# Laying the rows of five matmul operands without gaps in a one-core decoder layer

## The chip, the cores and the metric

The kernel runs on one NeuronCore of a Trainium2 chip. A core has a matrix engine (TensorE, "PE" in the profile, with its weight loads as "PEld"), a vector engine (VectorE, DVE), a scalar engine (ScalarE, ACT), a general engine (GpSimd, POOL), a synchronising engine that issues most transfers (SyncE, SP), and 16 DMA engines. On-chip memory (SBUF) has 128 partitions; matmul results go to PSUM, in banks of 512 float32 columns. The metric is the device time of one execution in microseconds.

## The reference

One decoder layer over 16 learned meta tokens and 256 tokens of width 2048, all in float32:

```python
h = jnp.concatenate([meta, x], axis=1)
h = h + hybrid_mixer(rmsnorm(h, norm_mix_g), w_in, ...)
h = h + squared_relu_mlp(rmsnorm(h, norm_mlp_g), w_ff1, w_ff2)
return rmsnorm(h, final_norm_g)[:, N_META:]
```

`hybrid_mixer` projects the normalised rows with `w_in` (13,336 columns: queries, keys and values of two branches, their gates, a forget gate). One branch is causal softmax attention with a forgetting term (8 heads of 128), the other a gated linear attention in chunks of 64 (4 heads, keys 256, values 512) with a normalisation by head and a SiLU gate. Each branch goes through its own output matrix and a sigmoid gate, the two are added, and `w_out` projects the sum:

```python
y = sigmoid(gate_fox) * (o_fox @ w_o_fox) + sigmoid(gate_gla) * (o_gla @ w_o_gla)
return y @ w_out
```

The MLP is `square(relu(xn @ w1)) @ w2` with 8192 hidden columns. The weights are most of the 289 MB that the kernel reads, and nearly all of the work is dense matrix products of 256 or 272 columns with them.

## The kernel before, in words

Everything is transposed: features lie on the 128 partitions, tokens along the free dimension. A vector of 2048 features is 16 row tiles of 128 partitions (`KT = 16`), and row tile k of an operand is the slice `[:, k, ...]` of one SBUF tile.

**Split operands.** A float32 number is cut into a high part, which the matmul type float32r (F32R) holds exactly, and a low part, the rest. An operand row tile holds its 256 high columns and then its 256 low columns, 512 in a row (`x[:, k]`). Weights are cut the same way. The product of one block of 128 output features is the function `gemm2`: for each of its 16 row tiles `mac2` issues two matmuls, the high weights against all 512 columns (L136) and the low weights against the 256 high columns (L137), all into one PSUM bank. The halves of the bank are added when it is read out. Each of these matmuls loads its own 128x128 weights first (PEld), while the matmul before it still runs.

**Weights.** `next_weights` fetches the next block of 128 columns in two halves of 512 KB (tile `raw`, SP's queue, L118), ACT copies each to the high part `whi` (L120) and DVE makes the low part `wlo` (L121), 1024 columns at a time. `raw`, `whi` and `wlo` have five buffers each. The blocks come in one fixed stream in the order of use, and a planner in the tile framework orders the instructions of each engine, from the order of the code.

**Operands.** The first operand, the normalised input, is the tile `x_row`. It holds 544 columns a row tile, `[meta high 16 | high 256 | low 256 | meta low 16]`; `x` is the 512 columns in the middle, `x_hi` the first 272 and `x_lo` the last 272. `gemm_all` multiplies all 272 token columns (L153 and L154 on `x_hi`, L155 on `x_lo` with its output 16 columns further on in PSUM). Five later operands come from the helper `operand`:

- `og` (L460, 16 row tiles), the output of the gated linear attention, and `x2` (L846), the normalised input of the MLP, both in the slot with tag "s2";
- `of` (L685, 8 row tiles, with `at=32`), the output of the softmax attention;
- `y` (L836), the gated sum, and `a` (L886), the squared ReLU of one quarter of the hidden columns, both in the slot with tag "s1", which `x_row` used before them.

The layout of such a tile is set by three lines:

```python
row = 2 * NT + 32                                       # 544
t = t[:, at:].rearrange("p (k r) -> p k r", r=row)
return t[:, :, 16 : 16 + 2 * NT].rearrange("p k (o t) -> p k o t", t=NT)
```

Row tiles are 544 columns apart, 2176 bytes, and each has its 512 columns after 16 unused ones and before 16 unused ones, as `x` has in `x_row`.

**Stages.** A first stage multiplies seven blocks while the input still arrives (`products`, L345 to L352), with the same row tile against several blocks in turn. Then come the four heads of the linear attention and the eight heads of the softmax attention, which read `x` and `x_hi`; then, for each pair of output blocks, gates on `x`, one block on `of` and two on `og`. `y` is split after that (`split_to`) and multiplied by `w_out`, and `x2` is written block by block as the residual grows. The MLP runs in four groups: 16 blocks on `x2` make one `a`, 16 blocks on `a` are added to the residual. The last four blocks of the last group are done in another order, so that the final normalisation of one half of the tokens can run beside the other half's products: first the low weights (L912), with the high weights kept in `whi_last` (tag "s2"), and then each half of 128 tokens with its high and low columns, 256 together (L928).

Of the kernel before, what the change touches and what calls it, by code (L numbers as in the profile page):

```python
# [8 lines left out]
F32R = mybir.dt.float32r  # L9
# [7 lines left out]
P = 128  # L17
# [3 lines left out]
NT = 256  # L21
# [44 lines left out]
def trunk(ctx: ExitStack, tc: tile.TileContext, hT, w_small, w_all, consts, w_alpha2, out):  # L66
# [3 lines left out]
    def nm(s):  # L70
        serial[0] += 1
        return f"{s}_{serial[0]}"
# [52 lines left out]
    def next_weights(keep_hi=None):  # L125
        c = chunk[0]
        chunk[0] += 1
        parts = []
        for i in range(2):
            hi, lo, step = weight_half(c, i, None if keep_hi is None else keep_hi[:, HK * i : HK * (i + 1), :])  # L130
            step(0, HK)
            parts.append((hi, lo))
        return lambda k: (parts[k // HK][0][:, k % HK, :], parts[k // HK][1][:, k % HK, :])
# [5 lines left out]
    def gemm2(w, x, k0=0, nk=KT):  # L139

        ps = bank(pg, "ps")
        for k in range(nk):
            hi, lo = w(k0 + k)
            mac2(ps, hi, lo, x[:, k], k == 0, k == nk - 1)
        issued()
        return ps
# [18 lines left out]
    def total(ps, t=None):  # L165

        b = tmp.tile([P, NT], F32, tag="evb", name=nm("evb"))
        nc.scalar.copy(b, ps[:, NT:512])  # L168
        if t is None:
            t = tmp.tile([P, NT], F32, tag="evt", name=nm("evt"), bufs=4)  # L170
        nc.vector.tensor_tensor(t, ps[:, 0:NT], b, op=ALU.add)  # L171
        return t
# [44 lines left out]

    def operand(pool, name, nk=KT, at=0, **kw):


        row = 2 * NT + 32
        t = pool.tile([P, at + nk * row], F32R, name=nm(name), **kw)
        t = t[:, at:].rearrange("p (k r) -> p k r", r=row)
        return t[:, :, 16 : 16 + 2 * NT].rearrange("p k (o t) -> p k o t", t=NT)


    h = keep.tile([P, KT, NA + 3], F32, name="h")
# [88 lines left out]
    for s in range(KT // 2):  # L316
# [5 lines left out]
        for kk in range(2):  # L322
            k = 2 * s + kk
# [15 lines left out]
        at = [(w[0][:, c], w[1][:, c]) for w, n in ((wa, 4), (wb, 3)) for c in range(n)]  # L339
# [118 lines left out]
    def og_tile():  # L458
        if not og_box:
            og_box.append(operand(keep, "og", tag="s2"))  # L460
        return og_box[0]
# [221 lines left out]
    branches = ExitStack()  # L683
    late = branches.enter_context(tc.tile_pool(name="late", bufs=1, reuse_waits="tile"))
    of = operand(late, "of", FOX_H, 32)  # L685
    negc = late.tile([P, FOX_H, NA], F32, name="negc")
    nc.gpsimd.dma_start(negc.rearrange("p h t -> p (h t)"), fdram.to_broadcast([P, FOX_H * NA]))
# [138 lines left out]
    for j0 in range(0, KT, 2):  # L826
        gates = ahead if j0 == 0 else [gate() for _ in range(4)]
        w = next_weights()
        for j in range(2):
            t = total(gemm2(w, of, k0=8 * j, nk=8))  # L830
            nc.vector.tensor_tensor(gates[2 * j], gates[2 * j], t, op=ALU.mult)
        for j in range(2):
            t = total(gemm2(next_weights(), og))
            nc.vector.tensor_tensor(t, gates[2 * j + 1], t, op=ALU.mult)
            nc.vector.tensor_tensor(yf[:, j0 + j, :], gates[2 * j], t, op=ALU.add)
    y = operand(keep, "y", tag="s1")  # L836
    for j in range(KT):
        split_to(y[:, j, 0, :], y[:, j, 1, :], yf[:, j, :])
# [220 lines left out]
```

## Time and profile before

| | |
|---|---|
| timed runs | 1597.07 us median of 3 (1596.95 to 1597.44) |
| span of the profiled execution | 1595.0 us |
| PE busy | 1585.0 us, 9812 matmuls |
| PEld busy | 1428.8 us |
| DVE, ACT, POOL busy | 1060.4, 790.8, 125.2 us |
| HBM read | 289.32 MB, 183 GB/s over the span |
| granted TensorE clock, mean | 0.998 |

The profile describes one execution, from its first instruction to its last; the timed runs count 2.1 us more than that span. A line of a group names the source line, the engine, the operation and the tiles (output, then inputs), the shape, how many there are, the sum of their durations, the mean of one in ns, and the idle time before them. In the chain and the timeline a row is a start, a length, and what ran. The ends of matmuls are modelled and overlap the next one, so durations of matmuls add up to more than the time they occupy; the starts give the pace. `x` in a group's name can be the tile `x` or the tile `x2`, since numbers in names are left out.

### The profile page before, as it was taken

The numbers are of one execution on the slowest core, as the hardware profiler recorded it, in microseconds if no ns is written. First come the engines' busy times: TensorE is split into PE (matmuls) and PEld (weight loads), VectorE is DVE, ScalarE is ACT, GpSimd is POOL, SyncE is SP. The second block draws the span as 40 slices with busy tenths as digits, with TensorE's granted clock in tenths as the row PEclk, the third lists the DMA queues.
The fourth block names the chain that finished last, engine by engine and source line by source line (L and its number), as shares of the span: only waits on it lengthen the run. The fifth ranks groups of instructions, "written<-read, shape, count | busy, mean of one in ns | idle before, by whom it ended". The sixth has DMA issues, their size and how long they took to land.

```text
span 1595.0 us, 25427 instructions
## 1 busy us (share of the span) xinstructions
PE 1585.0 (99%) x9812; PEld 1428.8 (90%) x9812; DVE 1060.4 (66%) x1659; ACT 790.8 (50%) x1271; POOL 125.2 (8%) x213
## 2 busy tenths in 40 slices
PE   9999999999999999999999999999999999999997
PEld 8999999999998888888888888888888888888887
DVE  7897757676655555555777776567655776567655
ACT  6665444454455444444555544444444444444563
POOL 6011000011100000000011000000000000000022
PEclk9999999999999999999999999999999999999999
DMA  9444545454445555555555555555555555555552
GB/s 323 156 164 155 180 157 183 167 188 164 159 167 181 191 186 189 189 191 187 186 195 186 188 193 187 188 191 190 187 190 190 186 189 193 186 188 193 186 183 97
DMA packets 86602, 293.09 MB, mean 184 GB/s; under 512 B 9112, under 2 KB 16800, under 8 KB 86352
## 3 DMA queue, kind: packets, MB, share of 16 engines
q1 hardware_dynamic: 85872, 289.62, 53.8%
q8 instruction: 77, 1.26, 0.3%
q0 software_dynamic: 176, 1.12, 0.2%
q10 hardware_dynamic: 432, 0.72, 0.1%
q14 instruction: 45, 0.37, 0.1%
HBM read 289.32 MB, written 2.11 MB: 183 GB/s over the span
## 4 chain that ended last, share of the span: by engine, by line
PE 99%; DMA 0%; issue 0%; POOL 0%; ACT 0%; DVE 0%; SPq 0%; POOLq 0%; ACTq 0%
PE ps L136 51%; PE ps L137 27%; PE psa L155 5%; PE psa L154 5%; PE psa L153 5%; PE ps L345 1%; PE ps L350 1%; PE ps L928 1%; PE pa L548 1%; PE ps L912 0%; DMA raw<-w_all_dram 0%; PE po L611 0%; POOL o L976 0%; PE po L188 0%; PE ps L348 0%
## 5 line engine op out<-in xcount | busy, mean ns | idle before, releaser
L121 DVE TENSOR_TENSOR wlo<-raw,whi 128x1024 fp32r<-128x1024 f32 x522 | 641.0, 1228 | 452.8 <-ACT whi L120 449.4
L120 ACT CAST whi<-raw 128x1024 fp32r<-128x1024 f32 x522 | 548.1, 1050 | 660.0 <-PE ps L136 493.1
L136 PE MATMUL ps<-x,whi 128*128 128x512 f32 x1952 | 683.8, 393 | 0.0
L137 PE MATMUL ps<-x,wlo 128*128 128x256 f32 x1952 | 548.5, 281 | 0.0
L136 PEld LDWEIGHTS ps<-x,whi 128*128 128x128 f32 x1952 | 366.1, 188 | 80.4
L137 PEld LDWEIGHTS ps<-x,wlo 128*128 128x128 f32 x1952 | 368.3, 189 | 0.1
L136 PE MATMUL ps<-a,whi 128*128 128x512 f32 x960 | 334.3, 392 | 0.0
L137 PE MATMUL ps<-a,wlo 128*128 128x256 f32 x960 | 269.1, 281 | 0.0
L136 PEld LDWEIGHTS ps<-a,whi 128*128 128x128 f32 x960 | 179.8, 188 | 39.9
L137 PEld LDWEIGHTS ps<-a,wlo 128*128 128x128 f32 x960 | 181.1, 189 | 0.3
L153 PE MATMUL psa<-x,whi 128*128 128x272 f32 x624 | 181.2, 290 | 0.0
L155 PE MATMUL psa<-x,whi 128*128 128x272 f32 x624 | 181.1, 290 | 0.0
L154 PE MATMUL psa<-x,wlo 128*128 128x272 f32 x624 | 179.4, 288 | 0.0
L153 PEld LDWEIGHTS psa<-x,whi 128*128 128x128 f32 x624 | 118.1, 189 | 0.4
L154 PEld LDWEIGHTS psa<-x,wlo 128*128 128x128 f32 x624 | 117.4, 188 | 0.0
L155 PEld LDWEIGHTS psa<-x,whi 128*128 128x128 f32 x624 | 117.2, 188 | 0.0
L136 PE MATMUL ps<-og,whi 128*128 128x512 f32 x256 | 89.6, 392 | 0.0
L136 PE MATMUL ps<-y,whi 128*128 128x512 f32 x256 | 89.1, 392 | 0.0
L854 POOL TENSOR_TENSOR acc<-acc,hsq 128x256 f32<-128x256 f32 x26 | 28.5, 1097 | 769.2 <-ACT hsq L853 769.2
L137 PE MATMUL ps<-og,wlo 128*128 128x256 f32 x256 | 71.9, 281 | 0.0
L137 PE MATMUL ps<-y,wlo 128*128 128x256 f32 x256 | 71.8, 281 | 0.0
L171 DVE TENSOR_TENSOR evt<-ps,evb 128x256 f32<-128x256 f32 x158 | 65.9, 418 | 0.5 <-ACT evb L168 0.5
(301 smaller groups left out, 1437.0 us busy)
## 6 DMA issues: line engine op xcount, KB each, us to landing
raw<-w_all_dram SPq DMA_DIRECT2D x537, 512.0 KB, 3.6
raw<-w_all_dram SPq DMA_DIRECT2D x8, 384.0 KB, 6.6
h<-hT_dram SPq DMA_DIRECT2D x8, 275.0 KB, 6.7
negc<-fdram POOLq DMA_DIRECT2D x1, 1088.0 KB, 8.0
out_dram<-o SPq DMA_DIRECT2D x2, 512.0 KB, 2.7
raw<-w_all_dram SPq DMA_DIRECT2D x2, 256.0 KB, 3.9
room<-w_small_dram SPq DMA_DIRECT2D x1, 320.0 KB, 7.4
out_dram<-o ACTq DMA_DIRECT2D x1, 320.0 KB, 3.1
```

Of the source, the lines that this page charges most:

```text
L120: nc.scalar.copy(hi[:, k, :], r)
L121: nc.vector.tensor_tensor(lo[:, k, :], r, hi[:, k, :].bitcast(F32), op=ALU.subtract)
L136: nc.tensor.matmul(ps, hi, x, start=first, stop=False)
L137: nc.tensor.matmul(ps[:, 0:NT], lo, x[:, 0, :], start=False, stop=last)
L153: nc.tensor.matmul(ps[:, 0:NA], hi, x_hi[:, k], start=(k == 0), stop=False)
L154: nc.tensor.matmul(ps[:, 0:NA], lo, x_hi[:, k], start=False, stop=(k == KT - 1))
L155: nc.tensor.matmul(ps[:, X_LO], hi, x_lo[:, k], start=False, stop=(k == KT - 1), skip_group_check=True)
L171: nc.vector.tensor_tensor(t, ps[:, 0:NT], b, op=ALU.add)
L345: nc.tensor.matmul(ps, hi, x[:, k], start=st, stop=False)
L350: nc.tensor.matmul(ps[:, 0:NT], lo, x[:, k, 0], start=False, stop=sp)
L548: nc.tensor.matmul(dst, k[:, a], q[:, a, :], start=(a == 0), stop=(a == 1))
L854: nc.gpsimd.tensor_tensor(acc, acc, sq, op=ALU.add)
```

## The change

The five operands keep their slots, but their row tiles now lie one behind the other, 512 columns (2048 bytes) apart, with nothing between them. The 32 spare columns for each row tile stay allocated at the tile's end. `at` still moves the first row of `of` by 32 columns. With the addresses that the tiles get, every row tile of the five now stands 448 bytes from the weight tiles, modulo 512; before, the row tiles of an operand stood 0, 128, 256 and 384 bytes from them in turn. `x_row` is not touched, nor is any instruction other than in its addresses.

```diff
     def operand(pool, name, nk=KT, at=0, **kw):
 
-
-        row = 2 * NT + 32
-        t = pool.tile([P, at + nk * row], F32R, name=nm(name), **kw)
-        t = t[:, at:].rearrange("p (k r) -> p k r", r=row)
-        return t[:, :, 16 : 16 + 2 * NT].rearrange("p k (o t) -> p k o t", t=NT)
+        t = pool.tile([P, nk * (2 * NT + 32)], F32R, name=nm(name), **kw)
+        return t[:, at : at + nk * 2 * NT].rearrange("p (k o t) -> p k o t", o=2, t=NT)
```

## The prediction

> **What bounds the kernel now.** I read the chain that ended last first, then the PE waits, then one long stretch of plain matrix products. The chain, by engine and by line, on the page:
>
> ```profile
> PE 99%; DMA 0%; issue 0%; POOL 0%; ACT 0%; DVE 0%; SPq 0%; POOLq 0%; ACTq 0%
> PE ps L136 51%; PE ps L137 27%; PE psa L155 5%; PE psa L154 5%; PE psa L153 5%; PE ps L345 1%; PE ps L350 1%; PE ps L928 1%; PE pa L548 1%; PE ps L912 0%; DMA raw<-w_all_dram 0%; PE po L611 0%; POOL o L976 0%; PE po L188 0%; PE ps L348 0%
> ```
>
> TensorE is the path from end to end, and 78% of it is the two matmuls of `mac2`, L136 (512 columns, high weights) and L137 (256 columns, low weights). The whole list of waits of that engine is three lines, 2.4 us together:
>
> ```profile
> PE warm L311 <- DVE ones L195: 1.3, 1, 1.3
> PE pn L952 <- ACT sq L933: 0.7, 1, 0.7
> PE ps L345 <- ACT whi L280: 0.4, 1, 0.4
> ```
>
> So no wait can be saved; only the pace of the matmuls can move the time. The stretch from 880 to 1560 us holds nothing but L136 and L137. Its busy times by engine (PE, PEld, DVE, ACT, POOL, then granted clock, DMA share, GB/s), and the matmul groups in it:
>
> ```profile
> 880.00:1560.00 680.00, 680.00 (x3907) 598.14 (x3906) 444.06 (x629) 321.28 (x456) 11.71 (x9) 1.00 0.56 189
> L136 PE MATMUL ps<-x,whi 128*128 128x512 f32 x999 | 348.2, 392 | 0.0
> L136 PE MATMUL ps<-a,whi 128*128 128x512 f32 x954 | 332.2, 392 | 0.0
> L137 PE MATMUL ps<-x,wlo 128*128 128x256 f32 x999 | 280.7, 281 | 0.0
> ```
>
> 999 + 954 = 1953 pairs in 680 us: 348.2 ns a pair. The durations 392 and 281 add up to 673, so each record is (673 - 348.2)/2 = 162 ns longer than the time until the next matmul starts. I therefore read any matmul duration as "start to next start, plus 162": L136 takes 230 ns, L137 119 (together 349). The clock is full (1.00), so the pace is not throttled. DVE, ACT and DMA are busy 65%, 47% and 56% of the stretch: if TensorE ran some per cent faster they would keep up.
>
> **The change, part by part.** Nothing is added, removed or reordered: every engine's list of instructions and waits is the same in both programs. What differs is where the rows of five tiles lie. The built programs place the weight tiles (`whi`, `wlo`) 128 bytes into a 512-byte period, and their rows are 512 bytes, so they stay there. The tiles `y`, `a`, `og`, `x2` begin 64 bytes into the period, `of` 448. Before, a row began 64 bytes in (128 more for `of`) and rows were 2176 bytes apart, so row k stood 128k bytes from the weights: 0, 128, 256, 384, 0 and so on. After, rows are 2048 bytes apart with no offset, so all stand at 64 - 128 = -64, that is 448. `x` is a tile of its own kind and keeps its places.
>
> The pairs that read the five tiles, first ones after 870 us (where "x" is `x2`), then the mixer's:
>
> ```profile
> L136 PE MATMUL ps<-x,whi x1024: 388/393/395, 871.0 to 1495.1; 128*128 128x512 f32 x171
> L136 PE MATMUL ps<-a,whi 128*128 128x512 f32 x960 | 334.3, 392 | 0.0
> L136 PE MATMUL ps<-og,whi 128*128 128x512 f32 x256 | 89.6, 392 | 0.0
> L136 PE MATMUL ps<-y,whi 128*128 128x512 f32 x256 | 89.1, 392 | 0.0
> L136 PE MATMUL ps<-of,whi 128*128 128x512 f32 x128 | 45.1, 393 | 0.0
> ```
>
> 1024 + 960 + 256 + 256 + 128 = 2624 pairs, 2624 x 348.2 ns = 913.7 us of the span. One nanosecond a pair is 2.6 us. That product is the whole sum; the question is its price.
>
> The trace of before has no 512-column matmul at distance 448, so I bound the price by the nearest rows. First, `x_hi` in `gemm_all`: its rows stand at 448, 64, 192, 320. Rows k = 12 and 13 of one such product, single instructions, 272 columns each (duration minimum/median/maximum):
>
> ```profile
> L153 PE MATMUL psa<-x,whi x1: 285/285/285, 286.7 to 286.7; 128*128 128x272 f32 x1
> L154 PE MATMUL psa<-x,wlo x1: 288/288/288, 286.9 to 286.9; 128*128 128x272 f32 x1
> L155 PE MATMUL psa<-x,whi x1: 292/292/292, 287.0 to 287.0; 128*128 128x272 f32 x1
> L153 PE MATMUL psa<-x,whi x1: 288/288/288, 287.1 to 287.1; 128*128 128x272 f32 x1
> L154 PE MATMUL psa<-x,wlo x1: 287/287/287, 287.2 to 287.2; 128*128 128x272 f32 x1
> L155 PE MATMUL psa<-x,whi x1: 289/289/289, 287.4 to 287.4; 128*128 128x272 f32 x1
> ```
>
> By distance: 448 gives 285 and 288, 0 gives 292, 64 gives 288 and 287, 128 gives 289. So 448 averages 286.5, the distances of before (multiples of 128) 290.5: 4 ns less a matmul. But L155 also writes PSUM 64 bytes further on, so this is an upper end of the gain: 8 ns a pair, 21 us.
>
> Second, runs of 256-column matmuls near the end, in the chain (start, length, count):
>
> ```profile
> 1562.51 5.68 PE ps L912 x48
> ...
> 1571.96 7.47 PE ps L928 x64
> ```
>
> L912 reads `a` against `wlo`, at multiples of 128: 5.68/48 = 118.3 ns. L928 reads `a` against `whi_last`, which begins 64 bytes into the period, so its distances are 64, 192, 320, 448: 7.47/64 = 116.7 ns. That is 1.6 ns less a matmul off the multiples of 128, with weights and rows in other absolute places than above.
>
> Third, against it: runs that stay at one distance for four matmuls, in the first stage (rows at 128, then 0, weights of other columns):
>
> ```profile
> 26.02 0.92 PE ps L345 x4
> 26.94 0.47 PE ps L350 x4
> 27.41 0.94 PE ps L345 x4
> 28.35 0.47 PE ps L350 x4
> ```
>
> (0.92 + 0.47 + 0.94 + 0.47)/8 = 350.0 ns a pair, 1.8 above the mixed rows.
>
> So the price lies between -8 and, at the cost of one bad distance for ever, the excess of 292 over the six rows' mean (288.2): 3.8 a matmul, +7.6 a pair. I take -1.6 a matmul, -3.2 a pair, from L912 against L928: these rows have the operands, the shape and the loads of weights of L137, and the single rows at 448 lie on the same side. 2624 x 3.2 = 8.4 us less.
>
> Edits that go together with it: L912 moves to 448 (64 x -1.6 = -0.1 us), and L928 moves to distance 0, since `whi_last` and `a` then both stand at 64 (128 x 1.6 = +0.2 us): nothing together. The ACT and DVE instructions that write the rows change addresses alone; TensorE waits for ACT 1.1 us in all, above, so whatever happens to them lies beside the matmuls. The pools keep their sizes but for `of`, 128 bytes shorter, which shifts its neighbours; the small matmuls are about 1% of the chain (L548 with L188 and L611 above, 16 us); I put them at nothing, and a tenth more or less on all of them would be 1.6 us either way.
>
> The span of the profiled execution is 1595.0 us; the timed runs have 1597.07 at the median, 2.1 us more for what lies around the span. 1595.0 - 8.4 = 1586.6 on the profile, about 1588.7 on the clock of the runs.
>
> **A rule against it.** "TensorE: Matmul & The Clock Gate" of the Trainium skill (Part 2, step-by-step) says that the engine reads the moving rows and the weights through two independent ports, and that loading the next weights takes no read bandwidth from the running matmul. By that rule the distance cannot matter and the time stays 1597. The rows above agree only in part: 285 to 292 for one shape at full clock is a spread by something, but it does not show that the two reads collide.
>
> **The rivals.** *No change.* If the spread is bookkeeping, no place is better. A duration here is a difference of two starts; a matmul that starts late lends its delay to the one before. The two triples above sum to 285 + 288 + 292 = 865 and 288 + 287 + 289 = 864, equal, though their distances differ: this speaks for it. Against it: 118.3 and 116.7 are means over long runs, where nothing can be lent. Time: 1597, within 3 us.
>
> *Slower.* What collides now in one row of four would collide in every one. Before, four distances take turns, and a bad one is paid once in four pairs; after, the engine settles into one relation of row and weights and pays or saves it 2624 times. The third fence is its price: +1.8 a pair, 4.7 us, 1601.8; at the worst distance seen, 7.6 a pair, 20 us, 1617. It decides from 1.2 ns a pair (3.2 us). For it: the only runs at a constant distance are the slower ones, and the 512-column shape never stood off a multiple of 128, so a cost of reading a long row from there has had no chance to show. Against it: neither of the two runs is at 448, and 448 has the shortest row of the six.
>
> **How the numbers follow.** 0.2% (3.2 us) is about what a measurement of this kernel can tell from no change. The forecast, faster by 3 to 21 us, gets 0.48: two kinds of rows in different absolute places point to it. Slower gets 0.36, since the step from four distances to one and from 272 to 512 columns is not covered by a row. No change gets 0.16, from the equal triples. The likeliest case alone is 1580 to 1593; with both signs holding much of the chance the range is 1580 to 1610, where the top leaves the dearest distance out and the bottom the full 8 ns a pair, about 0.1 each.
>
> **What would show it.** In the changed kernel's stretch from 880 to 1560 us the pairs should be 345 ns apart instead of 348.2 (some 18 more pairs in 680 us), with L136 near 390 and L137 near 279 by mean duration, and no difference left between one row and the next. Pairs of `x` in the mixer should stay as they are. L928 should move from 116.7 to about 118. The PE waits should stay at 2.4 us. I am wrong if pairs of `y`, `a`, `og` and `x2` are at or above 348 ns; if they stand at 350 or more, the constant distance is what costs, and if only L136 grows, it is the long row at an odd place.

## The result, and the profile after

The changed kernel takes 1610.12 us at the median (1609.51 to 1610.36) against 1597.03 us (1596.95 to 1597.44): a ratio of 1.0082, 95% interval 1.0069 to 1.0095. It is slower by 13.1 us. Its profiled execution has a span of 1608.3 us; before it was 1595.0 us, so the span shows the same 13.3 us.

The page's chain by engine, then the whole list of waits of TensorE (tile, line, what it waited for, us in total, times, longest), both of the changed kernel. Its lines below the helper stand three lower than before: L342 was L345, L909 was L912, L925 was L928.

```profile
PE 99%; DMA 0%; issue 0%; POOL 0%; ACT 0%; DVE 0%; SPq 0%; POOLq 0%; ACTq 0%
```

```profile
PE warm L308 <- DVE ones L195: 1.3, 1, 1.3
PE pn L949 <- ACT sq L930: 0.7, 1, 0.7
PE ps L342 <- ACT whi L277: 0.2, 1, 0.2
```

TensorE is still the whole path, and it waits 2.2 us where it waited 2.4. Nothing new makes it wait; it is its pace that fell. The same stretch as before, 880 to 1560 us, as a row of busy times by engine (PE, PEld, DVE, ACT, POOL, then granted clock, DMA share, GB/s):

```profile
880.00:1560.00 680.00, 680.00 (x3852) 590.59 (x3851) 436.97 (x622) 313.38 (x444) 8.94 (x7) 1.00 0.58 186
```

and the groups of matmuls in it (count, busy us, mean duration in ns, idle us before them):

```profile
L136 PE MATMUL ps<-x,whi 128*128 128x512 f32 x1008 | 356.4, 397 | 0.0
L136 PE MATMUL ps<-a,whi 128*128 128x512 f32 x917 | 323.9, 397 | 0.0
L137 PE MATMUL ps<-x,wlo 128*128 128x256 f32 x1008 | 283.2, 281 | 0.0
L137 PE MATMUL ps<-a,wlo 128*128 128x256 f32 x917 | 257.0, 281 | 0.0
```

1008 + 917 = 1925 pairs in 680 us are 353.2 ns a pair, where 1953 pairs were 348.2. The clock is full in both, and TensorE has no idle time before these matmuls in either. By the starts of the matmuls the extra 5.0 ns lie at 4.2 in L136 (235.0 ns to the next start, 230.8 before) and 0.8 in L137 (118.3, 117.5 before), and every row tile of `og`, `y`, `x2` and `a` has the same gaps. 2624 pairs x 5.0 ns = 13.1 us: that is the whole difference. The pairs on `x` keep 348.3 ns. Two of the chain's rows near the end (start, length, count), for the final blocks:

```profile
1575.47 5.66 PE ps L909 x48
...
1584.92 7.68 PE ps L925 x64
```

5.66/48 = 117.9 ns (118.3 before) and 7.68/64 = 120.0 ns (116.7 before): the first went from four distances to 448 and became slightly faster, the second from four distances to 0 and became slower.

### The profile page after: what moved, and what is told of

Read it like the earlier page. It is cut to its first block, busy times and chain, and to the rows that moved or that the text cites. A ratio compares the mean times of both kernels' runs of the same rounds, so it can differ in the third digit from the quotient of the medians.

```text
span 1608.3 us, 25427 instructions
## 1 busy us (share of the span) xinstructions
PE 1598.3 (99%) x9812; PEld 1430.4 (89%) x9812; DVE 1060.3 (66%) x1659; ACT 790.4 (49%) x1271; POOL 126.6 (8%) x213
## 4 chain that ended last, share of the span: by engine, by line
PE 99%; DMA 0%; issue 0%; POOL 0%; ACT 0%; DVE 0%; SPq 0%; POOLq 0%; ACTq 0%
PE ps L136 51%; PE ps L137 26%; PE psa L155 5%; PE psa L154 5%; PE psa L153 5%; PE ps L342 1%; PE ps L347 1%; PE ps L925 1%; PE pa L545 1%; PE ps L909 0%; DMA raw<-w_all_dram 0%; PE po L608 0%; POOL o L973 0%; PE po L188 0%; PE ps L345 0%
## 5 line engine op out<-in xcount | busy, mean ns | idle before, releaser
L136 PE MATMUL ps<-x,whi 128*128 128x512 f32 x1952 | 688.9, 396 | 0.0
L137 PE MATMUL ps<-x,wlo 128*128 128x256 f32 x1952 | 548.5, 281 | 0.0
L136 PEld LDWEIGHTS ps<-x,whi 128*128 128x128 f32 x1952 | 366.6, 188 | 85.1
L137 PEld LDWEIGHTS ps<-x,wlo 128*128 128x128 f32 x1952 | 367.3, 188 | 0.1
L136 PE MATMUL ps<-a,whi 128*128 128x512 f32 x960 | 339.0, 397 | 0.0
L137 PE MATMUL ps<-a,wlo 128*128 128x256 f32 x960 | 269.1, 281 | 0.0
L136 PEld LDWEIGHTS ps<-a,whi 128*128 128x128 f32 x960 | 180.2, 188 | 44.2
L137 PEld LDWEIGHTS ps<-a,wlo 128*128 128x128 f32 x960 | 180.2, 188 | 0.4
L136 PE MATMUL ps<-og,whi 128*128 128x512 f32 x256 | 90.8, 397 | 0.0
L136 PE MATMUL ps<-y,whi 128*128 128x512 f32 x256 | 90.4, 397 | 0.0
L137 PE MATMUL ps<-og,wlo 128*128 128x256 f32 x256 | 71.9, 281 | 0.0
L137 PE MATMUL ps<-y,wlo 128*128 128x256 f32 x256 | 71.8, 281 | 0.0
```

Source lines behind the costliest of these rows:

```text
L136: nc.tensor.matmul(ps, hi, x, start=first, stop=False)
L137: nc.tensor.matmul(ps[:, 0:NT], lo, x[:, 0, :], start=False, stop=last)
```

## The experiments

All of them change addresses alone, the places of the rows or of the weights, except the last, which also has four `raw` buffers in place of five (and a few copies of ScalarE in another order). In every trace TensorE runs the 9812 matmuls of the changed kernel in the same order. A time without a range is a single run. They share this edit of the helper; `place` gives for each tile the columns from one row tile to the next and the offset of the first:

```diff
     def operand(pool, name, nk=KT, at=0, **kw):
+        row, at = place[name]
         t = pool.tile([P, nk * (2 * NT + 32)], F32R, name=nm(name), **kw)
-        return t[:, at : at + nk * 2 * NT].rearrange("p (k o t) -> p k o t", o=2, t=NT)
+        off = at if row > 2 * NT else 0
+        t = t[:, at - off : at - off + nk * row].rearrange("p (k r) -> p k r", r=row)
+        return t[:, :, off : off + 2 * NT].rearrange("p k (o t) -> p k o t", t=NT)
...
-        a = operand(keep, "a", tag="s1")
+        a = operand(keep, f"a{g}", tag="s1")
```

`a0` to `a3` are the four groups of `a`. With the weights where the change has them, a packed `x2`, `og`, `y` or `a` with offset `at` stands 4 x at - 64 bytes from the high weights (modulo 512); `of` begins elsewhere and has an offset of its own. "Distance" below is row less weights; "settled" is a stage without its first two blocks of 16 pairs. Where no row is shown, a pace is the mean gap between starts of matmuls in the trace.

### Other constant distances

```diff
+    place = {'x2': (512, 16), 'og': (512, 32), 'y': (512, 48),
+             'a0': (512, 64), 'a1': (512, 80), 'a2': (512, 96), 'a3': (512, 112), 'of': (512, 32)}
```

> All five tiles stay packed, so each keeps one distance from the weights, but every tile gets another one: x2 at 0, og 64, y 128, the four a at 192, 256, 320 and 384, of stays at 448. Read by the pace of a pair (L136 plus L137) in each tile's stretch; before 348.3 ns, after 353.3. Theory 'long row at an odd place' (rows that do not begin at a multiple of 128 bytes): og, two of the a (192, 320) and of at 353, the others (x2, y, a at 256 and 384) at 348 to 350. Theory 'constant distance': all eight at 353. Theory 'only 448 collides': of 353, the others spread from 345 to 351.

It took 1604.94 us beside 1596.64 for the kernel before. Windows of 72 us (the last: 60), each within one stage, in the order `x2` (distance 0), `a0` (192), `x2` again, `a1` (256), `x2`, `a2` (320), `a3` (384); the first pair of numbers is PE's busy time and its matmuls:

```profile
885.00:957.00 72.00, 72.00 (x410) 62.45 (x409) 54.93 (x93) 35.22 (x53) 0.00 (x0) 1.00 0.59 192
975.00:1047.00 72.00, 72.00 (x409) 62.52 (x408) 42.14 (x54) 30.56 (x39) 0.00 (x0) 1.00 0.57 191
1062.00:1134.00 72.00, 72.00 (x410) 62.46 (x409) 51.01 (x78) 33.63 (x51) 0.00 (x0) 1.00 0.55 186
1155.00:1227.00 72.00, 72.00 (x417) 62.94 (x416) 43.20 (x56) 31.66 (x41) 0.00 (x0) 1.00 0.59 192
1240.00:1312.00 72.00, 72.00 (x417) 62.96 (x417) 51.63 (x78) 34.65 (x53) 0.00 (x0) 1.00 0.59 190
1332.00:1404.00 72.00, 72.00 (x410) 62.74 (x409) 42.72 (x54) 31.08 (x40) 0.00 (x0) 1.00 0.59 189
1509.00:1569.00 60.00, 60.00 (x344) 52.57 (x343) 33.08 (x41) 36.17 (x55) 11.93 (x9) 1.00 0.57 188
```

Read the matmul count: 409 or 410 in 72 us are 352 ns a pair, 417 are 345; they read a little over 1 ns low, because a matmul that only reaches into the window is counted too. The starts give 353.3 for 192 and 320, 351.1 for 384, and 346.7 for 256. So a constant distance need not be dear, and a row off the multiples of 128 is not the cause by itself, since 384, a multiple of 128, is dear too. The surprise is `x2`: the same places of rows and weights modulo 512, the same instructions, 353.3 in its first two stages and 346.7 in the third (the fourth, not shown, is back at 353.3). At distance 0 the engine can run in either of two ways, and keeps through a stage the one that it fell into.

### Is it the distance, or the row's own place?

The weights move by 64 bytes, and the rows of `x2`, `og`, `y` and `a` stay as in the experiment above:

```diff
     tmp = ctx.enter_context(tc.tile_pool(name="tmp", bufs=2))
+    wp.tile([P, 16], F32, tag="pad", name="pad", bufs=1)
```

> As the first, with the weight tiles 64 bytes further on. The rows keep their absolute places (x2 128, og 192, y 256, a 320, 384, 448, 0) and every distance falls by 64: x2 at 448, og 0, y 64, a at 128, 192, 256, 320. If the row's own place decides, each tile keeps its pace of the first run, and x2 stays below 350. If the distance decides, paces follow the distance: x2 takes 353 as all tiles did at 448 after the change, og takes what x2 took at 0. Under 'constant distance' all stay at 353.

It took 1607.4 us. The stages `x2` (now at 448), `a0` (128), `a1` (192) and `a2` (256):

```profile
890.00:962.00 72.00, 72.00 (x409) 62.52 (x408) 53.85 (x88) 34.48 (x53) 0.00 (x0) 1.00 0.58 189
980.00:1052.00 72.00, 72.00 (x412) 63.07 (x411) 40.95 (x51) 30.31 (x39) 0.00 (x0) 1.00 0.59 193
1155.00:1227.00 72.00, 72.00 (x410) 62.57 (x409) 42.65 (x53) 31.09 (x41) 0.00 (x0) 1.00 0.58 188
1336.00:1408.00 72.00, 72.00 (x418) 62.97 (x417) 43.59 (x55) 31.82 (x41) 0.00 (x0) 1.00 0.58 191
```

`x2` has gone to 353.3 with its gaps of 235 and 118, the very gaps of the changed kernel, with rows that stand on a multiple of 128 bytes: what matters is the row against the weights. `a1` at 192 has the same gaps. `a0`, `a1` and `a2` now show what the tile at that distance showed above, 351.1, 353.3 and 346.7, though their rows have not moved. One pair of readings does not fit: at distance 64 and 320 the pace was 353 above and is 349 here.

### Keep the gaps, lose the multiples of 128

The change did two things to the distances: it made them constant, and it took them off the multiples of 128. Here row tiles are 544 columns apart as before the change, but begin 64 bytes earlier, so that the distances are 448, 64, 192, 320 in turn:

```diff
+    place = {'x2': (544, 0), 'og': (544, 0), 'y': (544, 0), 'a0': (544, 0), 'a1': (544, 0),
+             'a2': (544, 0), 'a3': (544, 0), 'of': (544, 0)}
```

> The gaps of before, every row 64 bytes earlier: distances 448, 64, 192, 320 in turn. If the cost of the change is the constant distance alone, 1597 (pairs 348.3). If it is being off the multiples of 128 alone, 1610 (353.3). From x2 in the third run: 350.0, so 2624 x 1.7 = +4.5: 1601.5, a third of the change's cost.

1601.44 us (1601.13 to 1602.03), ratio 1.003 (1.0018 to 1.0042): slower than before, by about a third of the change. The settled pace is 350.0 ns in every stage that reads `y`, `x2` or `a`, that is +1.7 of the +5.0; 2624 x 1.7 = 4.5 us of the 4.7 measured. The other 3.3 ns come with holding one distance, 448. A stage of `x2` and one of `a0`:

```profile
885.00:957.00 72.00, 72.00 (x413) 62.98 (x413) 54.95 (x91) 34.63 (x52) 0.00 (x0) 1.00 0.59 193
975.00:1047.00 72.00, 72.00 (x413) 62.99 (x412) 41.02 (x52) 30.58 (x39) 0.00 (x0) 1.00 0.60 193
```

Ten L136 of `a0` (durations minimum, median, maximum; first and last start):

```profile
L136 PE MATMUL ps<-a,whi x10: 392/394/397, 999.6 to 1002.8; 128*128 128x512 f32 x10
```

They alternate between 392 and 397, 230 and 234 ns to the next start. The short ones are the rows whose own distance is 192 or 448, the long ones those at 64 or 320. With the distance held at 448 or 192 all rows take the long form, 235. A single row's gap in a run of mixed distances therefore does not tell what its distance costs: here the long form comes on the rows behind those at 448 and 192.

### Odd strides

```diff
+    place = {'x2': (544, 0), 'og': (528, 0), 'y': (544, 8), 'a0': (520, 0), 'a1': (544, 4),
+             'a2': (512, 8), 'a3': (512, 4), 'of': (544, 16)}
```

> Rows with gaps again, in several ways, weights where they were: x2 2176 bytes apart but 64 bytes earlier than before (distances 448, 64, 192, 320 in turn); og 2112 apart (steps of 64); y 2176 apart at 480, 96, 224, 352; one a 2080 apart (steps of 32), one 2176 apart at 464, 80, 208, 336; two a packed at a constant 480 and 464; of 2176 apart as before. 'Odd place': x2 353, og about 351 (half its rows), of 348. 'Constant distance': x2, og and of at 348, the two packed a at 353. 'Only 448': x2 349 to 350 (a quarter of its rows), og 349.

1603.98 us. No stride repaired it: `x2` (448, 64, 192, 320 in turn) 350.0 ns, `og` (rows 2112 bytes apart) 349.0, `y` (480, 96, 224, 352) 351.6, `a0` (2080 apart) 350.8, `a2` (constant 480) 353.3, `a3` (constant 464) 350.0. `a1` (464, 80, 208, 336) settled at 356.7, the dearest of all runs, so 353.3 is not a ceiling. Places between the multiples of 64 bytes brought nothing in this run.

### High and low weights apart

So far `whi` and `wlo` stood at the same place in the period. A pad between the two moves the low weights alone, here by 192 bytes:

```diff
         hi = wp.tile([P, HK, P], F32R, tag="whi", name=nm("whi"))
+        if c0 == k0 == 0:
+            wp.tile([P, 48], F32, tag="pad", name="pad", bufs=1)
         lo = wp.tile([P, HK, P], F32R, tag="wlo", name=nm("wlo"))
...
+    place = {'x2': (512, 0), 'a0': (512, 48), 'a1': (512, 64), 'a2': (512, 80), 'a3': (512, 112),
+             'og': (512, 16), 'y': (512, 32), 'of': (512, 80)}
```

> Rows packed; the low weights stand 192 bytes further on than before, the high ones where they were, so a row has two distances, to the high weights that L136 multiplies with (and that load beside L137) and to the low ones (that load beside L136). Tiles by (high, low) distance: x2 448/256, og 0/320, y 64/384, the four a 128/448, 192/0, 256/64, 384/192, of 320/128. Theory 'the matmul collides with the load that runs beside it': L136 goes by the low distance: about 231 to 232 in x2 and 235 in the a at 128/448. Theory 'the matmul's own weights': L136 goes by the high distance: 235 in x2, 230.6 in that a. Theory 'place of the row alone': L136 is 235 in x2, og, as in rows at 64 and 192 bytes.

1600.34 us (1596.73 before). The stages `y` (64 from the high weights, 384 from the low), `a0` (128 and 448) and `a1` (192 and 0):

```profile
795.00:867.00 72.00, 72.00 (x417) 63.44 (x416) 54.33 (x68) 40.93 (x68) 11.92 (x13) 1.00 0.61 196
972.00:1044.00 72.00, 72.00 (x417) 63.37 (x416) 43.37 (x55) 31.70 (x42) 0.00 (x0) 1.00 0.58 190
1150.00:1222.00 72.00, 72.00 (x414) 63.32 (x413) 42.33 (x53) 32.09 (x41) 0.00 (x0) 1.00 0.58 188
```

While L136 streams its rows, the low weights are loaded beside it. If that load were what 448 collides with, `a0`, at 448 from the low weights, would have an L136 of 235 ns; it has 228. `a1`, at 192 from the high ones, has 232. The groups of the two (mean durations 391 and 395, where the change has 397):

```profile
L136 PE MATMUL ps<-a,whi 128*128 128x512 f32 x209 | 72.4, 391 | 0.0
L136 PE MATMUL ps<-a,whi 128*128 128x512 f32 x207 | 72.4, 395 | 0.0
```

In these stages the distance from the high weights weighs more, but it does not decide alone: at 64 the pace is now 346.7, and it was 349 to 353 with the low weights at the same distance.

### The low weights 64, 128 and 256 bytes on

The same pad, in three sizes (16, 32 and 64 columns), with distances from the high weights of 128 (`x2`), 0 (`og`), 64 (`y`) and 192, 256, 320, 384 (`a0` to `a3`):

```diff
+            wp.tile([P, 16], F32, tag="pad", name="pad", bufs=1)
...
+    place = {'x2': (512, 48), 'og': (512, 16), 'y': (512, 32),
+             'a0': (512, 64), 'a1': (512, 80), 'a2': (512, 96), 'a3': (512, 112), 'of': (512, 16)}
```

> As the fourth run (rows packed, two distances), with the low weights only 64 bytes further on. By (high, low) distance: x2 128/64, og 0/448, y 64/0, the four a 192/128, 256/192, 320/256, 384/320, of 448/384. The fourth run spoke for the matmul's own weights: by that, L136 orders by the high distance alone (shortest at 128, 384 and 64, 320, longest at 192, 448 and 0, 256), whatever the low one: x2 and a at 384 near 228, a at 192 and of near 232. If the low distance counts instead (the load beside L136), a at 320/256 and y at 64/0 are like the 256 rows (230 to 235) and a at 256/192 is 235. Every pair pattern is to repeat on a multiple of 6.67 ns, as all before did.

> Low weights 128 bytes further on. By (high, low): x2 128/0, og 0/384, y 64/448, the four a 192/64, 256/128, 320/192, 384/256, of 448/320. 'Own weights': x2 and a at 384/256 near 228, a at 192/64 and of 448/320 near 232. 'Load beside': y 64/448 and a 320/192 at 235.

> Low weights 256 bytes further on; by the runs with one place for both, distances repeat every 256 bytes, so this should be as if they were not apart: x2 128/384 at 351.1 a pair, og 0/256 and a 256/0 at 346.7 or 353.3, a 192/448 and of 448/192 at 353.3, a 384/128 at 351.1, y and a at 320 at 353; x at 348.3.

Times: 1592.58, 1603.65 and 1604.17 us (1596.81 before). In the first of them the stages `y` (64 from the high, 0 from the low weights), `a0` (192 and 128), `a1` (256 and 192), `a2` (320 and 256):

```profile
795.00:867.00 72.00, 72.00 (x426) 63.67 (x425) 55.03 (x70) 41.85 (x69) 12.71 (x13) 1.00 0.61 201
970.00:1042.00 72.00, 72.00 (x410) 63.03 (x409) 42.65 (x55) 30.55 (x41) 0.00 (x0) 1.00 0.58 190
1148.00:1220.00 72.00, 72.00 (x418) 63.69 (x417) 43.63 (x55) 31.77 (x41) 0.00 (x0) 1.00 0.58 191
1327.00:1399.00 72.00, 72.00 (x426) 63.73 (x425) 43.23 (x55) 31.79 (x40) 0.00 (x0) 1.00 0.60 198
```

426 matmuls in 72 us: 340.0 ns a pair by the starts, less than anything before. The theories on record did not survive the pads of 64 and 128 bytes. With 128 bytes, 'own weights' said 228 ns for the L136 of `x2` (128 from the high weights), and it has 233; 'load beside' said 235 for that of `y` (448 from the low ones), and it has 229. In the third, where the low weights move by 256 bytes, each tile has the pace of the run without a pad at its distance (`a0` 353.3, `a1` 346.7, `x2` and `a3` 351.1), so the pattern repeats every 256 bytes. With that, the runs fill this table (settled ns a pair; distances modulo 256; two numbers where stages differ):

| from high \ from low | 0 | 64 | 128 | 192 |
|---|---|---|---|---|
| 0 | 346.7 or 353.3 | 346.7, 351.1 | 346.7, 350.0 | 346.7 |
| 64 | **340.0** | 349 or 353.3 | 346.7 | 346.7 |
| 128 | 352.0 | 346.7 | 351.1 | 346.7 |
| 192 | 350.0, 353.3 | 351.6 to 353.3 | 350.4, 353.3 | **353.3** |

448 is 192 modulo 256, and before and after the change the two kinds of weights stand at one place: the change put all 2624 pairs into the lower right cell, the only one of the diagonal that was 353.3 (352.3 to 353.3 with the short stages of `of`) wherever it was met. The row for 192 is the only one without a pace below 350.0; the column for 192 is cheap in the other three rows, so it is the pair of distances that counts.

### The changed kernel at 256 instead of 448, two ways

First the rows move (offset 80 for all, 112 for `of`), then the weights move under rows that stay where the change put them (a pad of 48 columns ahead of both):

```diff
+    place = {'x2': (512, 80), 'og': (512, 80), 'y': (512, 80), 'a0': (512, 80), 'a1': (512, 80),
+             'a2': (512, 80), 'a3': (512, 80), 'of': (512, 112)}
```

> All five tiles packed, 320 bytes further on than in the change, so all at the constant distance 256. 'Distance decides': pairs settle at 346.7 ns as in the one a at 256 of the first run, 2624 x (346.7 - 348.3) = -4.2 us: 1592.8; if some tile stays in the slower state that the first two blocks there showed (353), each of its pairs costs 6.6 more and the time may reach 1610. 'Any constant distance': 1610.

```diff
     tmp = ctx.enter_context(tc.tile_pool(name="tmp", bufs=2))
+    wp.tile([P, 48], F32, tag="pad", name="pad", bufs=1)
...
+    place = {'x2': (512, 0), 'og': (512, 0), 'y': (512, 0), 'a0': (512, 0), 'a1': (512, 0),
+             'a2': (512, 0), 'a3': (512, 0), 'of': (512, 112)}
```

> Rows exactly where the change puts them (64 bytes into the 512-byte period, packed); the weight tiles 192 bytes further on instead, so the distance is 256, and x moves to 320, 448, 64, 192. 'Distance decides': pairs of the five at 346.7, those of x at 350.1 as in the second run (928 x 1.8 = +1.7 us): 1597 - 4.2 + 1.7 = 1594.5. 'Place of the row': 353.3 as in the change, 1610 to 1612.

1601.0 us (1600.32 to 1601.2), ratio 1.0026 (1.0016 to 1.0037), and 1603.34 us (1603.24 to 1603.36), ratio 1.0041 (1.0026 to 1.0056). Both are faster than the change and slower than before, because of the two ways of running. Of the first, `a0` and `a1`; then of the second, the same two:

```profile
972.00:1044.00 72.00, 72.00 (x409) 62.49 (x408) 41.88 (x55) 30.78 (x39) 0.00 (x0) 1.00 0.60 193
1155.00:1227.00 72.00, 72.00 (x418) 62.97 (x417) 41.75 (x53) 30.83 (x39) 0.00 (x0) 1.00 0.60 196
```

```profile
970.00:1042.00 72.00, 72.00 (x417) 62.97 (x417) 41.90 (x54) 30.83 (x39) 0.00 (x0) 1.00 0.58 189
1155.00:1227.00 72.00, 72.00 (x410) 62.46 (x409) 41.56 (x52) 29.51 (x38) 0.00 (x0) 1.00 0.59 193
```

Stages with equal addresses modulo 512 and equal code run at 353 or at 346.7, and which of them is which differs between the runs. In both, `a0` and `a2` go one way and `a1` and `a3` the other. By means of 15 pairs in turn, a stage begins at the pace of the stage before it: the second to fourth stages of `x2` keep what `a` had, and in both runs the pace switches within the first two blocks of the first `x2` and of `a1`, `a2` and `a3`, and not in `a0`. The two runs switch at the same points of the program and differ in the pace that they came with (`y` at 346.7 in the first, 353.3 in the second). The stages of `x2` in the first experiment, at distance 0, fit this too: the one at 346.7 follows the `a1` at 346.7. With rows in the change's own place, pairs can take 346.7: the row's place is not what made the change slow.

### The best cell for all five, and then for `x` too

```diff
+            wp.tile([P, 16], F32, tag="pad", name="pad", bufs=1)
...
+    place = {'x2': (512, 32), 'og': (512, 32), 'y': (512, 32), 'a0': (512, 32), 'a1': (512, 32),
+             'a2': (512, 32), 'a3': (512, 32), 'of': (512, 48)}
```

> The packed rows of the change, but the five tiles 128 bytes further on and the low weights 64 bytes further on: all five tiles 64 bytes from the high weights and 0 from the low ones, the place at which y (16 blocks) and a 320/256 tile settled at 340.0 ns in the run with 64 bytes between the weights. 'The two distances set the pace': 2624 x (340.0 - 348.3) = -21.8 us, x slightly dearer (928 x 0.3 = +0.3 us) and gemm_all 624 x 2.6 ns = +1.6 us: about 1577. 'Packed rows cost by themselves, and these two tiles were lucky in how they started': some tiles at 346.7 or 353, 1590 or more.

```diff
-RAW = 5
+RAW = 4
...
-    x_row = keep.tile([P, KT, 2 * NA], F32R, tag="s1", name="x")
+    x_row = keep.tile([P, 9344], F32R, tag="s1", name="x")
+    x_row = x_row[:, 16 : 16 + KT * 576].rearrange("p (k r) -> p k r", r=576)[:, :, 0 : 2 * NA]
```

> As the one before, with the rows of x 2304 bytes apart instead of 2176 and 64 bytes further on, so that x too stands at 64/0 and 320/256 alone; the space comes from four raw buffers instead of five. 'The two distances set the pace': x's 928 pairs go from 348.6 to 340.0, 8 us less than the run before, 1569, if four raw buffers still feed the engines; rival: the missing buffer makes ACT wait for transfers, and TensorE waits of several us appear.

The first, packed rows 64 bytes from the high and 0 from the low weights: 1577.66 us (1577.57 to 1577.75) against 1597.01, ratio 0.9879 (0.9863 to 0.9895). Its groups from 880 to 1540 us:

```profile
L136 PE MATMUL ps<-x,whi 128*128 128x512 f32 x990 | 336.8, 389 | 0.0
L136 PE MATMUL ps<-a,whi 128*128 128x512 f32 x952 | 323.7, 389 | 0.0
L137 PE MATMUL ps<-x,wlo 128*128 128x256 f32 x990 | 273.2, 276 | 0.0
L137 PE MATMUL ps<-a,wlo 128*128 128x256 f32 x951 | 261.9, 276 | 0.0
```

990 + 952 = 1942 pairs in 660 us: 339.9 ns, with durations of 389 and 276 where the change has 397 and 281. The sum closes: 2624 x 8.1 ns = 21.3 us gained on the five tiles; `gemm_all`, whose low weights the pad moved too, went from 376.5 to 379.1 ns for its three matmuls and the pairs on `x` from 348.3 to 348.6, together about 1.9 us lost; 19.4 expected, 19.4 measured.

The second also spreads the rows of `x` to 2304 bytes (a multiple of 256) and puts them at the same distances; to make room, four buffers `raw` have to do in place of five (`whi` and `wlo` keep five). 1568.84 us (1568.46 to 1569.64), ratio 0.9823 (0.9809 to 0.9837): the fastest kernel here. A stretch of the MLP (PE first), and TensorE's waits:

```profile
880.00:1500.00 620.00, 620.00 (x3648) 549.60 (x3647) 414.91 (x589) 294.50 (x416) 4.25 (x3) 1.00 0.59 194
```

```profile
PE warm L316 <- DVE ones L195: 1.3, 1, 1.3
PE pn L957 <- ACT sq L938: 0.7, 1, 0.7
```

1824 pairs in 620 us are 339.9 ns, and four `raw` buffers are enough, since TensorE waits 2.0 us in all. The time was forecast (1569), but in part by luck: the pairs on `x` came down to 343.0 and not to 340.0, which is 5.2 us (928 x 5.6) of the 8 expected, and `gemm_all`, which the expectation left out, went from 379.1 to 373.5, 3.5 us (624 x 5.6), and made up for it.

## Why the prediction was wrong

**What held.** TensorE is the path from end to end, and the change moves the time only by the pace of 2624 pairs: 2624 x 5.0 ns is the whole difference. Nothing else moved the time, as the prediction put it: the waits went from 2.4 to 2.2 us and the pairs on `x` kept 348.3 ns. L912 and L928 moved the ways that were forecast, but not by the 1.6 ns: L912 fell by 0.4 (118.3 to 117.9), L928 rose by 3.3 (116.7 to 120.0). "Start to next start, plus 162" is confirmed at the new pace: (397 + 281 - 353.2)/2 = 162.

**The step that failed** is the price: -1.6 ns a matmul "off the multiples of 128", taken from L912 against L928 and from single rows of `gemm_all`. It measured +4.2 on L136 and +0.8 on L137, +5.0 a pair where -3.2 was forecast.

- The single rows ("448 gives 285 and 288, 0 gives 292") were read as prices of distances. The run with the gaps kept shows the rows at 448 and 192 as the shorter ones (230 ns) among mixed distances, while the same distance, held at both high and low weights, costs 235. The prediction had named the reason itself, in its rival of no change: a matmul that starts late lends its delay to the one before, so a gap belongs to the sequence and not to the row. That objection struck at its own evidence and was spent on another forecast.
- L912 against L928 did compare long runs. But in both runs the distance changed from row to row, so they say nothing of a distance that is held, which is what the change makes of it. Held, they took 117.9 at 448 and 120.0 at 0.
- The distances were all taken against one set of weights. The runs show that a pair is ordered by two distances, from the high and from the low weights, with a period of 256; 448 from both is the cell that was 353.3 wherever it was met.

**The rival that came true** is the slower one: "the engine settles into one relation of row and weights and pays or saves it 2624 times" is what the trace shows, to the nanosecond. Its other half, that one of the four distances of before is the bad one, is not: 448 was not among them. That the change would settle into one distance was right; the price, +1.8 a pair from the run of L345 and L350 at distances 128 and 0, was too small. Only those rows of before held a distance for several matmuls, and only they had the right sign. Its other end, 7.6 a pair, lay above the 5.0 measured. The time came out a hair above the range's top of 1610.0: the range had left the dearest distance out.

**The rival of no change** had beside it the Trainium skill, "TensorE: Matmul & The Clock Gate" (Part 2, step-by-step), which states two independent read ports, one for the moving rows and one for the weights. The prediction inferred from it that places cannot matter, and the measurement decides against that: the same instructions at full clock take 340.0 to 356.7 ns a pair by addresses alone. The same page (Part 1, "Wait — 56ns, not 53.3ns?") gives the gap of back-to-back matmuls as columns / 2.4 GHz + 2.5 ns; an estimate from it for 512 and 256 columns is 215.8 + 109.2 = 325 ns, and the best pair measured here stands at 226 + 114 = 340, 15 ns above it. The estimate is worked out from the columns alone; no run here shows whether the 15 ns come from addresses, from the weights that each matmul loads, or from something else.

**What stays open** is which reads meet, and whether reads that meet are the reason at all. That the pace follows the two distances is shown by moving rows and weights apart from each other. That rows and weights are in each other's way while both are read is argued from it, and no run here takes the loads of weights away from beside the matmuls. The load beside L136 is not the one that 448 spoils by itself. Why the diagonal at 64 is 349 in some stages and 353 in others, and why the pace at 256 switches at the start of some stages and is handed on at others, is not settled either.

## What to carry to other kernels

Where TensorE is the whole path, the places of its operands modulo 256 bytes are worth a table of short runs: here the spread is 340 to 357 ns a pair, nearly 5%, at no cost in instructions, and one pad between two weight buffers, with the rows packed to fit it, gave 1.2%. Price an address by a long run that holds it, never by single gaps within a mixture, since a late start is charged to its neighbour. A change that makes a varying relation constant stakes the time on one value of it; measure that value held, because the mixture need not be the mean of its members: 448, 64, 192 and 320 in turn took 350.0 ns, and held, with the weights at one place, they took 353.3, or 349 to 353.3 for 64 and 320.

## What the runs showed of the hardware

- The pace depends on the distances of the moving rows from the high and from the low weights, modulo 256 bytes, and on the two together: 340.0 ns a pair at (64, 0), 353.3 at (192, 192), 346.7 at (64, 192).
- Settled paces fall on a grid of 6.67 ns: 340.0, 346.7 and 353.3 are 51, 52 and 53 of it for one pair, 700.0 and 713.3 (the 350.0 and 356.7 of the other patterns) 105 and 107 for two. Others are on it only over three pairs (348.9 and 351.1), four (348.3) or five (352.0). The traces show the steps, not what makes them.
- At distances of 0 and 256 the same code at the same addresses modulo 512 runs at 346.7 or 353.3. A stage takes over the pace of the stage before it or switches within its first two blocks, and then keeps to one pace to its end. A stage of 256 pairs that chose the other way would move the time by 1.7 us (256 x 6.7); the repeated runs of the two kernels at 256 lie within 0.9 and 0.1 us, so the outcome seems to repeat from run to run.
